# Paired heads in mixer 1, joint chunk operands and no filler matmuls in mixer 2, and a feed-forward whose last two output units run context tokens first

## The chip, the cores and the metric

The kernel runs on one core of one Trainium2 chip. The metric is the device time of one execution in microseconds. Before the change the median of three runs is 2691.66 us (2684.7 to 2692.46). Each core has TensorE (PE in the profile, with PEld for its weight loads), VectorE (DVE), ScalarE (ACT), GpSimd (POOL), SyncE (SP, which here issues DMAs), and DMA engines.

## The reference, cut to what matters

The model has four kinds of layer; the depth is 2, so two are computed: layer 0 (a bidirectional Mamba-2 mixer, then a dense SwiGLU) and layer 1 (a bidirectional RWKV-7 mixer, then eight SwiGLU experts, two per token). 256 context tokens and 256 latent tokens run through the same weights; only the latent tokens are returned.

```python
# Mamba-2, per direction, chunk of 128 tokens, G=4 groups x E=8 heads x P=64
seg = cum[:, :, :, None] - cum[:, :, None, :]
decay = jnp.exp(jnp.where(lower, seg, -jnp.inf))
cb = jnp.einsum('bcign,bcjgn->bcijg', cm, bm)
w = cb[..., None] * decay * dt[:, :, None]
y = jnp.einsum('bcijge,bcjgep->bcigep', w, x)          # "py" in the kernel
y = y + jnp.einsum('bcign,bcgepn->bcigep', cm, s_prev) * jnp.exp(cum)[..., None]

# SwiGLU and what follows it
f = (jax.nn.silu(gu[..., :F]) * gu[..., F:]) @ w_out
x = x + m[5] * f                                       # context and latent have their own m
h = _rmsnorm(x, norm1_g[1]) * (1 + m[1]) + m[0]        # mixer 2 begins

# RWKV-7, 16 heads of 64, per direction, one token at a time in the reference
sa = jnp.einsum('bhvk,bhk->bhv', S, kk_t)
S = S * w_t - sa * b_t + v_t * k_t
y_t = jnp.einsum('bhvk,bhk->bhv', S, r_t)
```

## The kernel before, in words

Activations lie with 128 features on the partitions and 512 tokens in a row: columns 0 to 255 are context, 256 to 511 latent. A large projection takes fp32 weights from HBM (`wraw`), splits them into a high and a low part (ACT cast, L206; a subtraction on DVE or POOL, L207), and runs three matmuls per tile (`mm3`, L212 to L214). Every other fp32 matmul, and so each of those that this change touches, is two records in the profile. The instructions are written as Python loops and coroutines (`weave` takes turns among them); a scheduler then orders each engine's list by its own timeline and by when tile buffers come free. So the order of the loops is not the order on an engine.

Mixer 1 (59 to 478 us) interleaves, group by group, the input projection of later features, the depthwise convolution on DVE (`cy`, L461), and the chunk computation in `mix`. There, for each pair of heads, `py` gets 128 x 512 values: per head and direction PE builds the segment sums (`pbc`, L542 and L543), ACT takes the exponential (`E`, L548), DVE multiplies by `cb` (`W`, L550), and four matmuls (L553) with 64 output rows add one chunk each. Before, the head is the outer loop, so sixteen records with the same half of the output stand in a row. `ZE = (G,)` sends the low splits of the z weights to POOL.

After the output projection and the first part of the feed-forward comes its second half (`hf == 1`): four output units n of 256 features, each over eleven k tiles and all 512 tokens. `Squares` then sums the squares of X, `rows` makes the row `rbx` of reciprocal root mean squares, and mixer 2's norm starts from it (L829, L830).

Mixer 2 (945 to 1657 us) has stages named for what runs together: A builds operands for chunks of 64 tokens in a direction (features with decay factors, `BK`; the Gram matrices `C`, L1077 and L1080; transposes `BT`, L1089), T inverts the triangular systems (`invert`), S scans. D0 and D1 are the directions; a first digit 0 is context (four chunks a direction), 1 is latent. Before, `BK` is two zero-padded tiles per slot, one per parity of the heads: 128 partitions by 4 by 128, of which 64 partitions carry data per half; so the writes L1060 and L1061 come in halves of 64 partitions. `invert` gets `warm=(2, 4)` in the stage A01T00: `spin` (L1116) then puts a 128 x 128 matmul whose result nobody reads between the small ones.

## Time and profile before

| | before |
|---|---|
| median of 3 runs | 2691.66 us |
| profiled execution | 2704.16 us |
| its span | 2702.3 us |
| PE busy | 2499.3 us (92%) |
| DVE busy | 2070.4 us (77%) |
| ACT busy | 1455.4 us (54%) |
| POOL busy | 416.1 us (15%) |
| mean granted clock of TensorE | 0.934 |

The profiled execution is 12.5 us above the median. Its 40 slices are 67.6 us long each. Read the page first by slices: the MoE (1658 us to the end) has PE and the DMA engines full and nothing of it is changed; the stages before it differ from one another, so every share has to be read per stage.

### The profile page before, as it was taken

The page shows a single profiled execution, that of the slowest core. Times are in us where ns is not written, and L with a number is a line of the kernel's source. Part 1 is how long each engine was busy: PE and PEld are TensorE (multiplying, and loading weights), DVE is VectorE, ACT ScalarE, POOL GpSimd, SP SyncE. Part 2 cuts the span into 40 slices and gives each one's busy share as a digit, 9 for nine tenths or more (in the row PEclk, how much of TensorE's full clock was granted, in tenths as well). Part 3 has the DMA queues.
Part 4 walks back from the last instruction along what each step waited for, and adds up shares of the span by engine and source line. Part 5 has one row for each costly group of instructions (what it writes and reads, how often), then busy time and mean ns, then how long its engine had stood idle before and what let it go on. Part 6 is the DMA issues. An engine that isn't in the chain of part 4 may idle for free. (4 is left out here: it accounts for less than half of the span.)

```text
span 2702.3 us, 43164 instructions
## 1 busy us (share of the span) xinstructions
PE 2499.3 (92%) x16810; PEld 2043.9 (76%) x16810; DVE 2070.4 (77%) x3118; ACT 1455.4 (54%) x2290; POOL 416.1 (15%) x506
## 2 busy tenths in 40 slices
PE   7999999999999968768977898999999999999997
PEld 4777776778888867558866687788788788878875
DVE  5777788667454377778696745999899899989997
ACT  4444446333222265336343334878787778778775
POOL 1122132110000156224453221000000000000001
PEclk9999999999999978577887877999999999999998
DMA  7322231335554231012110116699899899989983
GB/s 260 114 86 88 78 102 53 132 110 196 177 196 160 65 110 48 1 42 95 41 63 10 57 34 249 262 360 362 326 372 357 330 362 368 358 320 363 372 340 152
DMA packets 99207, 511.54 MB, mean 189 GB/s; under 512 B 11648, under 2 KB 19072, under 8 KB 55216
## 3 DMA queue, kind: packets, MB, share of 16 engines
q1 hardware_dynamic: 97520, 506.52, 51.1%
q8 instruction: 134, 2.20, 0.3%
q10 hardware_dynamic: 1472, 2.16, 0.3%
q14 instruction: 81, 0.66, 0.1%
HBM read 506.54 MB, written 2.10 MB: 188 GB/s over the span
## 5 line engine op out<-in xcount | busy, mean ns | idle before, releaser
L1734 DVE TENSOR_TENSOR wlo<-wraw,whi 128x1024 fp32r<-128x1024 f32 x662 | 798.4, 1224 | 71.3 <-ACT whi L1733 50.6
L1733 ACT CAST whi<-wraw 128x1024 fp32r<-128x1024 f32 x662 | 694.3, 1051 | 209.2 <-PE gu L214 112.0
L213 PE MATMUL gu<-wlo,xg 128*128 128x512 f32 x896 | 355.7, 397 | 1.5 <-DVE wlo L1734 0.7
L214 PE MATMUL gu<-whi,xg 128*128 128x512 f32 x896 | 350.3, 391 | 0.0
L212 PE MATMUL gu<-whi,xg 128*128 128x512 f32 x896 | 336.8, 392 | 1.1 <-ACT xg L1753 0.9
L206 ACT CAST whi<-wraw 128x1024 fp32r<-128x1024 f32 (+2 forms) x126 | 129.5, 1028 | 229.8 <-PE acc L213 216.4
L207 DVE TENSOR_TENSOR wlo<-wraw,whi 128x1024 fp32r<-128x1024 f32 (+2 forms) x110 | 131.7, 1198 | 106.3 <-ACT whi L206 106.2
L213 PEld LDWEIGHTS gu<-wlo,xg 128*128 128x128 f32 x896 | 168.8, 188 | 42.4 <-DVE wlo L1734 5.8
L212 PEld LDWEIGHTS gu<-whi,xg 128*128 128x128 f32 x896 | 168.7, 188 | 38.2 <-ACT xg L1753 1.6
L214 PEld LDWEIGHTS gu<-whi,xg 128*128 128x128 f32 x896 | 168.9, 188 | 31.6
L213 PE MATMUL y<-wlo,HT 128*128 128x512 f32 x448 | 179.1, 400 | 2.3 <-DVE wlo L1734 2.1
L212 PE MATMUL y<-whi,HT 128*128 128x512 f32 x448 | 177.1, 397 | 3.0 <-DVE xg L1754 3.0
L214 PE MATMUL y<-whi,HT 128*128 128x512 f32 x448 | 176.8, 395 | 0.0
L1808 POOL TENSOR_TENSOR wraw<-yx,SH 128x512 f32<-128x512 f32 x4 | 7.5, 1879 | 1025.4 <-DVE yx L1804 1025.4
L212 PE MATMUL acc<-h2hi,whi 128*128 128x512 f32 x352 | 137.3, 393 | 3.4 <-ACT h2hi L343 3.4
L213 PE MATMUL acc<-h2lo,whi 128*128 128x512 f32 x352 | 137.7, 391 | 0.0
L212 PE MATMUL acc<-hhi,whi 128*128 128x512 f32 (+1 forms) x328 | 135.8, 414 | 0.8 <-ACT whi L206 0.8
L214 PE MATMUL acc<-h2hi,wlo 128*128 128x512 f32 x352 | 135.0, 391 | 0.9 <-DVE wlo L207 0.9
L213 PE MATMUL acc<-hlo,whi 128*128 128x512 f32 (+1 forms) x328 | 134.1, 409 | 0.0
L214 PE MATMUL acc<-hhi,wlo 128*128 128x512 f32 (+1 forms) x328 | 133.8, 409 | 0.0
L305 POOL TENSOR_TENSOR sqa<-sqa,sq 128x512 f32<-128x512 f32 (+1 forms) x35 | 46.8, 1338 | 536.0 <-issue 311.9
L777 POOL TENSOR_TENSOR wlo<-wraw,whi 128x512 fp32r<-128x512 f32 (+1 forms) x69 | 86.1, 1257 | 150.3 <-ACT whi L776 138.9
(575 smaller groups left out, 5550.6 us busy)
## 6 DMA issues: line engine op xcount, KB each, us to landing
wraw<-in_w_mi_dram SPq DMA_DIRECT2D x219, 1024.0 KB, 4.9
wraw<-in_w_mo_dram SPq DMA_DIRECT2D x112, 1024.0 KB, 4.9
wraw<-in_w_modT_dram SPq DMA_DIRECT2D x56, 512.0 KB, 4.1
wraw<-in_w_ffi_dram SPq DMA_DIRECT2D x44, 512.0 KB, 3.6
wraw<-in_w_mod_dram SPq DMA_DIRECT2D x40, 512.0 KB, 4.5
wraw<-in_w_mb_dram SPq DMA_DIRECT2D x40, 512.0 KB, 4.3
wraw<-in_w_mbo_dram SPq DMA_DIRECT2D x16, 512.0 KB, 3.5
wraw<-in_w_ffo_dram SPq DMA_DIRECT2D x16, 512.0 KB, 3.5
```

The costliest lines, as they stand in the source:

```text
L206: S.copy(hi, raw)
L207: eng[q % len(eng)].tensor_sub(lo, raw, hi.bitcast(F32))
L212: PE.matmul(o, whi, xhi, start=start, stop=False)
L213: PE.matmul(o, whi, xlo, start=False, stop=False)
L214: PE.matmul(o, wlo, xhi, start=False, stop=stop)
L305: G.tensor_add(self.acc, self.acc, sq)
L777: self.eng[self.n % len(self.eng)].tensor_sub(lo, raw, hi.bitcast(F32))
L1733: S.copy(hi, raw[:, k:k + 2, :])
L1734: V.tensor_sub(lo, raw[:, k:k + 2, :], hi.bitcast(F32))
L1808: G.tensor_mul(xf[:, tt, 512 * n:512 * n + 512], fs, fg[:, 512 * n:512 * n + 512])
```

## The change

Four things change. In `mix` the direction becomes the outer loop: for both heads `E` and `W` are computed first (four W buffers in place of two), and then, chunk by chunk, the matmuls of head 0 and head 1 alternate, one with output partitions 0 to 63 and one with 64 to 127. Besides, the z weights' low splits go to DVE. In the feed-forward the last two of the four output units run in halves: context columns of unit 2, then of unit 3, then latent columns of both; sums of squares and the row are kept per half. In mixer 2, `BK` becomes one joint tile of 128 x 4 x 2 x 64 without padding: `BK[:, :, 0]` and `[:, :, 1]` are written by one instruction each on all partitions, the Gram matmuls and the transposes work on 64 x 64 blocks (transposes become matmuls with the identity), and `dc` is written by ACT from the cumulative sum instead of copied by DVE. In `invert` the filler matmuls go.

```diff
     class Squares:
-        def __init__(self, pool, n=NT):
+        def __init__(self, pool, n=NT, tag=""):
...
-        XE, ZE = (V,), (G,)
+        XE, ZE = (V,), (V,)
...
                 py = bank("py", 1)
-                for e in range(2):
-                    h = hf + 2 * m + e
-                    for d in range(2):
+                for d in range(2):
+                    Ws = []
+                    for e in range(2):
+                        h = hf + 2 * m + e
                         pbc = bank("pbc", 2)
...
-                        W = mt.tile([128, NT], F32, name="W")
+                        W = mt.tile([128, NT], F32, name="W", bufs=4)
                         V.tensor_mul(W, E, cb)
-                        for c in range(4):
-                            sl = slice(128 * c, 128 * c + 128)
+                        Ws.append(W)
+                    for c in range(4):
+                        sl = slice(128 * c, 128 * c + 128)
+                        for e in range(2):
                             PE.matmul(py[64 * e:64 * e + 64, sl], xdt[d][:, c, 128 * m + 64 * e:128 * m + 64 * e + 64],
-                                      W[:, sl], start=d == 0 and c == 0, stop=d == 1 and c == 3,
+                                      Ws[e][:, sl], start=d == 0 and c == 0, stop=d == 1 and c == 3,
                                       skip_group_check=True)
...
-        xsq = Squares(rowp)
+        xsq = {j: Squares(ft, 256, f"_{j}") for j in range(2)}
...
-            for n in range(4):
+            for n, part in [(n, HALF) for n in range(4 if hf == 0 else 2)] + \
+                    [(n, (x,)) for x in (HALF if hf else ()) for n in (2, 3)]:
                 mod_some(2 if hf == 0 else 0)
-                o = [acc(), acc()]
-                accumulate(o, wsplit(T["w_ffo"][hf, n]), lambda k: hid[k], 0, NH)
+                ts = slice(part[0][0].start, part[-1][0].stop)
+                o = [acc()[:, ts], acc()[:, ts]]
+                accumulate(o, wsplit(T["w_ffo"][hf, n]), lambda k: [t[:, ts] for t in hid[k]], 0, NH)
...
-        xsq.rows(D, rbx)
+                if hf and n == 3:
+                    xsq[j].rows(D, rbx[:, sl])
...
+            S.activation(un.dc[d][:, :, c:c + 1], cum[:, :, end:end + 1], AF.Exp, scale=-0.3032655)
...
-            V.tensor_copy(un.dc[d][:, :, c:c + 1], Dp[:, :, last:last + 1])
...
-            for par in range(2):
-                r, b0 = ROWS[par], 64 * par
-                V.scalar_tensor_tensor(BK[par][r, :, b0:b0 + 64], ta[r, :, cl], 0.5, Di[r], op0=ALU.mult, op1=ALU.mult)
-                G.tensor_mul(BK[par][r, :, 64 - b0:128 - b0], kd[r, :, cl], Di[r])
+            V.scalar_tensor_tensor(BK[:, :, 0], ta[:, :, cl], 0.5, Di, op0=ALU.mult, op1=ALU.mult)
+            G.tensor_mul(BK[:, :, 1], kd[:, :, cl], Di)
...
+        def side(BK, par, h, z):
+            return BK[ROWS[par], h, z ^ par, :]
...
-                    if j:
-                        PE.matmul(g[par][:, h, :], BK[par][:, h, :], KR[:, h, :], start=True, stop=True)
-                    else:
-                        for z in range(2):
-                            PE.matmul(g[par][ROWS[z], h, :], BK[par][:, h, 64 * z:64 * z + 64], KR[:, h, :],
-                                      start=True, stop=True)
+                    for z in range(2):
+                        PE.matmul(g[par][ROWS[z], h, :], side(BK, par, h, z), KR[ROWS[par], h, :], start=True, stop=True)
...
-                    PE.transpose(t[par][:, 64 * h:64 * h + 64], BK[par][ROWS[par], h, :],
-                                 ident[ROWS[par], ROWS[par]])
+                    for z in range(2):
+                        PE.matmul(t[par][ROWS[z], 64 * h:64 * h + 64], side(BK, par, h, z),
+                                  ident[ROWS[par], ROWS[par]], start=True, stop=True)
...
-    def invert(tp, un, zbank, slots={}, warm=(0, 0)):
+    def invert(tp, un, zbank, slots={}):
...
-                if warm[0] and n % warm[0] == 0:
-                    spin(zb[:, 256:], zp[:, d, n, 0:16].unsqueeze(2).to_broadcast([128, 16, 8]))
...
-            weave((invert(tp, D0, misc, warm=(2, 4)), 1), *stages(tp, r01, F, D1, 1, bks, (("gr", "xu"), ("acc", "xu")), always))
+            weave((invert(tp, D0, misc), 1), *stages(tp, r01, F, D1, 1, bks, (("gr", "xu"), ("acc", "xu")), always))
```

How the order on the engines changes is shown at three places. The first is PE in mixer 1, at one `py` group (`xdt0` and `xdt1` are the two directions, the W numbers buffers of the decay products). Before:

```order
L553 MATMUL py_843<-W_852,xdt0_677 64x128 x4
L542 LDWEIGHTS ehb_316
L542 MATMUL pbc_886<-parts1_389,ehb_316 128x512
L553 MATMUL py_843<-W_866,xdt1_678 64x128 x4
L543 LDWEIGHTS identb_83
L543 MATMUL pbc_886<-maskb_85,identb_83 128x512
```

and such a group in the changed kernel, whose lines are numbered four higher there:

```order
L557 MATMUL py_761<-W_770,xdt0_677 64x128
L557 MATMUL py_761<-W_780,xdt0_677 64x128
L557 MATMUL py_761<-W_770,xdt0_677 64x128
L557 MATMUL py_761<-W_780,xdt0_677 64x128
L557 MATMUL py_761<-W_770,xdt0_677 64x128
L525 MATMUL misc_723<-xw_721,btm_586 128x256
L557 MATMUL py_761<-W_780,xdt0_677 64x128
L525 MATMUL misc_729<-xw_727,btm_586 128x256
L557 MATMUL py_761<-W_770,xdt0_677 64x128
L557 MATMUL py_761<-W_780,xdt0_677 64x128
```

Four matmuls of one head stood in a row; now the two heads (two W buffers) take turns, and two other matmuls stand between members of one direction.

The second place is PE in the inversion of D0, stage A01T00 (M and T are the solver's tiles, `cst` the identity; L1116 is the filler). Before:

```order
L1116 MATMUL ms<-T,cst 128x128
L1197 MATMUL ms<-M_9366,T 32x16 x8
L1116 MATMUL ms<-T,cst 128x128
L1197 MATMUL ms<-M_9366,T 32x16 x8
L1116 MATMUL ms<-T,cst 128x128
```

and after, where L1196 is the same solve and L1017 and L1018 are low-rank projections of direction D1:

```order
L1196 MATMUL ms<-M_9613,T 32x16 x18
L1017 MATMUL xu<-hw_7701,l_9297 128x128
L1018 MATMUL xu<-ha_7703,l_9297 128x128
L1196 MATMUL ms<-M_9613,T 32x16 x2
L1017 MATMUL xu<-hw_7702,l_9297 128x128
L1018 MATMUL xu<-ha_7704,l_9297 128x128
L1196 MATMUL ms<-M_9613,T 32x16 x13
```

The fillers are gone, and eight pairs of D1's projections, which came behind the solve, moved into its first phase.

The third place is DVE at the end of the feed-forward (`rst` and `rbx` make the norm's row, `sq` is the norm's first product). Before:

```order
L317 RECIPROCAL rst<-rst 128x4
L323 COPY rbx<-misc 128x512
L777 TENSOR_TENSOR wlo<-wraw,whi 128x512
L699 COPY rbl<-rbx 128x256
L829 TENSOR_TENSOR sq<-X,rbx 128x256 x2
```

and after, at the second (latent) half's row:

```order
L317 RECIPROCAL rst_7640<-rst_7640 128x2
L704 TENSOR_SCALAR keep<-c_7662 128x2
L709 TENSOR_TENSOR hrk<-c_7662,vec 128x128
L323 COPY rbx<-misc 128x256
L711 TENSOR_SCALAR hrk<-hrk 128x128
L832 TENSOR_SCALAR modA<-mods_93 128x8
L837 TENSOR_TENSOR sq<-X,rbx 128x256 x2
L707 COPY rbl<-rbx 128x256
```

The context half's row is made ten rows ahead of these, and the latent half's here; the norm's first product (L829, now L837) still stands behind the second `rbx`, but ahead of the copy to `rbl` and of a weight split.

## Rows read from the trace of the kernel before

**Rows 1.** the page's span, and the granted clock in 40 slices.

```profile
span 2702.3 us, 43164 instructions
...
PEclk9999999999999978577887877999999999999998
```

**Rows 2.** busy time (records) of each engine by stretch, then granted clock, DMA share, GB/s.

```profile
104.00:200.00 96.00, 95.56 (x525) 70.63 (x524) 70.27 (x125) 42.33 (x96) 18.99 (x16) 1.00 0.23 77
200.00:300.00 100.00, 100.00 (x573) 77.31 (x573) 78.02 (x140) 49.85 (x119) 25.29 (x21) 1.00 0.24 85
300.00:400.00 100.00, 99.14 (x523) 73.80 (x522) 80.28 (x126) 42.49 (x92) 27.87 (x20) 1.00 0.27 90
400.00:478.00 78.00, 69.55 (x414) 51.60 (x414) 64.01 (x119) 43.31 (x116) 19.39 (x18) 1.00 0.18 62
1034.00:1117.00 83.00, 56.64 (x702) 49.53 (x698) 73.67 (x174) 44.13 (x128) 39.59 (x61) 0.86 0.06 20
1115.40:1153.20 37.80, 37.80 (x578) 28.99 (x578) 15.44 (x29) 7.59 (x16) 7.67 (x12) 0.50 0.01 2
...
1340.00:1400.00 60.00, 46.52 (x433) 40.91 (x433) 50.43 (x94) 25.89 (x73) 37.45 (x51) 0.89 0.13 45
1428.00:1446.60 18.60, 15.35 (x559) 14.00 (x560) 5.47 (x10) 5.97 (x13) 4.77 (x11) 0.54 0.02 4
1445.00:1535.00 90.00, 75.84 (x1133) 66.23 (x1132) 62.52 (x142) 40.45 (x112) 28.47 (x46) 0.88 0.02 6
```

**Rows 3.** PE's timeline in mixer 1: start, us from first start to last end.

```profile
209.76 1.96 PE L553 MATMUL py<-W,xdt 128*64 128x128 f32 x16
```

**Rows 4.** PE's timeline in the scan of mixer 2.

```profile
1319.03 0.69 PE L1242 MATMUL acc<-Q,BT 128*64 128x64 f32 x16
```

**Rows 5.** groups of PE up to 402 us: records, busy us, mean ns.

```profile
L553 PE MATMUL py<-W,xdt 128*64 128x128 f32 x352 | 46.6, 278 | 0.0
```

**Rows 6.** groups of all engines in mixer 1, 104 to 478 us.

```profile
L461 DVE SCALAR_TENSOR_TENSOR cy<-cv,cwh,cy 128x512 f32<-128x512 f32 x80 | 69.4, 869 | 1.1
...
L553 PE MATMUL py<-W,xdt 128*64 128x128 f32 x512 | 67.7, 278 | 1.3 <-DVE xdt L511 1.3
...
L207 POOL TENSOR_TENSOR wlo<-wraw,whi 128x1024 fp32r<-128x1024 f32 x13 | 34.5, 2652 | 44.1 <-ACT whi L206 44.1
...
L207 DVE TENSOR_TENSOR wlo<-wraw,whi 128x1024 fp32r<-128x1024 f32 x21 | 26.4, 1256 | 8.2 <-ACT whi L206 8.2
```

**Rows 7.** the convolution's line: ns min/median/max.

```profile
L461 DVE SCALAR_TENSOR_TENSOR cy<-cv,cwh,cy x96: 653/748/2944, 59.4 to 401.5; 128x512 f32<-128x512 f32 x96
```

**Rows 8.** busy time by stretch, matmuls of 512 columns, then of 256.

```profile
900.00:920.00 20.00, 20.00 (x90) 16.56 (x89) 5.37 (x8) 4.38 (x6) 3.87 (x3) 1.00 0.33 107
1240.00:1245.00 5.00, 5.00 (x44) 5.00 (x44) 2.14 (x5) 2.57 (x8) 1.89 (x2) 1.00 0.35 105
```

**Rows 9.** DVE's timeline behind the feed-forward.

```profile
948.10 0.69 DVE L323 COPY rbx<-misc 128x512 f32<-128x512 f32 x1 [1.21 <-PE misc L322]
...
949.52 1.34 DVE L699 COPY rbl<-rbx 128x256 f32<-128x256 f32 x1
950.78 0.75 DVE L829 TENSOR_TENSOR sq<-X,rbx 128x256 f32<-128x256 f32 x2
```

**Rows 10.** PE's timeline there.

```profile
956.57 0.80 PE L799 MATMUL gr<-mxh,whi 128*128 128x256 f32 x2 [8.50 <-ACT mxh L866]
```

**Rows 11.** the filler matmuls' line: ns min/median/max.

```profile
L1116 PE MATMUL ms<-T,cst x32: 421/501/582, 1115.4 to 1131.8; 128*128 128x128 f32 x32
```

**Rows 12.** groups of DVE in A00, 1034 to 1117 us.

```profile
L1060 DVE SCALAR_TENSOR_TENSOR BK<-ta,cum 64x256 f32<-64x256 f32 x22 | 14.6, 663 | 1.0 <-ACT cum L1045 0.6
...
L1053 DVE COPY dc<-Dp 128x4 f32<-128x4 f32 x11 | 4.2, 385 | 0.0
```

**Rows 13.** groups of A10 to S10A11, 1340 to 1535 us.

```profile
L1060 DVE SCALAR_TENSOR_TENSOR BK<-ta,cum 64x256 f32<-64x256 f32 x30 | 17.3, 576 | 0.4
...
L1053 DVE COPY dc<-Dp 128x4 f32<-128x4 f32 x15 | 7.9, 525 | 1.2 <-ACT Dp L1044 1.2
```

More of the change, by code (lines that the diff above doesn't have):

```diff
@@ L287, in tile_backbone @@
     class Squares:
-        def __init__(self, pool, n=NT):
-            self.pool, self.n, self.first, self.late = pool, n, True, []
-            self.acc = pool.tile([128, n], F32, name="sqa")
+        def __init__(self, pool, n=NT, tag=""):
+            self.pool, self.n, self.first, self.late, self.tag = pool, n, True, [], tag
+            self.acc = pool.tile([128, n], F32, name="sqa" + tag)
         def add(self, src, late=False):
@@ L299, in add @@
                 return
-            sq = self.pool.tile([128, self.n], F32, name="sq", bufs=2)
+            sq = self.pool.tile([128, self.n], F32, name="sq" + self.tag, bufs=2)
             S.activation(sq, src, AF.Square)
@@ L314, in rows @@
                               stop=i == len(parts) - 1, skip_group_check=True)
-            r = self.pool.tile([128, n], F32, name="rst")
+            r = self.pool.tile([128, n], F32, name="rst" + self.tag)
             S.activation(r, ss[:, :n], AF.Sqrt, scale=1.0 / width, bias=epsc)
@@ L661, in tile_backbone @@
                 hid.append((hi, lo))
-            for n in range(4):
+            for n, part in [(n, HALF) for n in range(4 if hf == 0 else 2)] + \
+                    [(n, (x,)) for x in (HALF if hf else ()) for n in (2, 3)]:
                 mod_some(2 if hf == 0 else 0)
-                o = [acc(), acc()]
-                accumulate(o, wsplit(T["w_ffo"][hf, n]), lambda k: hid[k], 0, NH)
+                ts = slice(part[0][0].start, part[-1][0].stop)
+                o = [acc()[:, ts], acc()[:, ts]]
+                accumulate(o, wsplit(T["w_ffo"][hf, n]), lambda k: [t[:, ts] for t in hid[k]], 0, NH)
                 for m in range(2):
-                    for sl, j in HALF:
-                        V.scalar_tensor_tensor(X[:, 2 * n + m, sl], o[m][:, sl], mcol(0, 5, 2 * n + m, j),
-                                               X[:, 2 * n + m, sl], op0=ALU.mult, op1=ALU.add)
-                    if hf:
-                        xsq.add(X[:, 2 * n + m, :], n == 3)
-        xsq.rows(D, rbx)
+                    for sl, j in part:
+                        V.scalar_tensor_tensor(X[:, 2 * n + m, sl], o[m][:, sl.start - ts.start:sl.stop - ts.start],
+                                               mcol(0, 5, 2 * n + m, j), X[:, 2 * n + m, sl], op0=ALU.mult, op1=ALU.add)
+                        if hf:
+                            xsq[j].add(X[:, 2 * n + m, sl], n == 3)
+                if hf and n == 3:
+                    xsq[j].rows(D, rbx[:, sl])
     dump("x2", X)
@@ L997, in stage @@
         o = 1 - d
-        last = 64 if d == 0 else 0
         gr, ms = (lambda: bank(tags[0], 2)), (lambda: bank(tags[1], 2))
@@ L1044, in decays @@
             S.activation(Dp[:, :, o:o + 64], cum, AF.Exp, scale=-0.3032655)
+            end = 63 * o
+            S.activation(un.dc[d][:, :, c:c + 1], cum[:, :, end:end + 1], AF.Exp, scale=-0.3032655)
             S.activation(cum, cum, AF.Exp, scale=0.3032655)
@@ L1112, in stage @@
             yield from grams(c, BK, 2 * i + d)
-    def spin(o, x):
-        PE.matmul(o[:, :x.shape[1] * x.shape[2]], ident, x, start=True, stop=True)
-    def invert(tp, un, zbank, slots={}, warm=(0, 0)):
+    def invert(tp, un, zbank, slots={}):
         def tile_(name, n):
@@ L1206, in invert @@
             for n in range(16):
-                if warm[1] and n % warm[1] == 0 and n < 13:
-                    spin(z[:, 32 * n:], TB[d][:, n, :].unsqueeze(2).to_broadcast([128, 32, 4]))
                 for par in range(2):
@@ L1220, in invert @@
             for n in range(16):
-                if warm[1] and n % warm[1] == 0 and n < 13:
-                    spin(z[:, 32 * n:], T32[d][:, n, :].unsqueeze(2).to_broadcast([128, 32, 4]))
                 for par in range(2):
@@ L1308, in operand_tiles @@
     def operand_tiles(tp):
-        t = [[tp.tile([128, 2, 4, 128], F32, name=f"BK{d}{i}") for i in range(2)] for d in range(2)]
-        for d in t:
-            for x in d:
-                for par in range(2):
-                    G.memset(x[:, par], 0.0)
-        return [[[x[:, par] for par in range(2)] for x in d] for d in t]
+        return [[tp.tile([128, 4, 2, 64], F32, name=f"BK{d}{i}") for i in range(2)] for d in range(2)]
     def stages(tp, rp, F, un, nb, bks, tags, ready, l2=None):
```

4 lines of the change are left out of this document (2 added, 2 removed).

## The prediction

> **What bounds the kernel now.** I read the profiled execution first by the granted clock in slices, then stage by stage in a table of windows, then single lines on the engine that the table names. The span is 2702.3 us and the execution 2704.2 [rows 1]. The clock's slices stand at nine tenths or more everywhere but in slices of 945 to 1657 us, mixer 2, and in the last one; that is the first sign that mixer 2 is a chain of short steps and mixer 1 is not. The windows say it exactly [rows 2]. In mixer 1, from 104 to 400 us, PE is busy 95.56 of 96, 100 of 100 and 99.14 of 100 us at clock 1.00: PE itself is the bound there, and only what it executes can be shortened. DVE comes next, 70.27, 78.02 and 80.28 us. In the last 78 us of mixer 1 PE has 8.45 us free. In A00 (1034 to 1117) DVE leads with 73.67 of 83 us, PE has 56.64. In the inversion of D0 (1115.4 to 1153.2) PE is busy in all of its 37.80 us, but at clock 0.50, the lower level of 1.2 GHz, whereas the inversion of the same form for latent chunks (1428 to 1446.6) takes 18.60 us. In A10 DVE has 50.43 of 60 us; in S10A11 PE leads with 75.84 of 90, DVE has 62.52.
>
> **Paired heads.** Sixteen records of 128 columns that write the same half of the output take 1.96 us from first start to last end [rows 3]; with a duration of 0.28 for the last one (the mean, 278 ns, [rows 5]) that is 1.68/15 = 112 ns from start to start, one after the other. In mixer 2's scan, sixteen records of 64 columns that alternate between the two halves of the output take 0.69 us [rows 4]. By the column, one after the other, these would need 15 x 56 = 840 ns before the last one's own duration; all together took less, so a pair runs side by side. The layout of a pair in the changed `py` (128 rows, two times 64 output rows) is the same as there. So a pair of 128-column records should take about 112 ns and not 224: 56 ns less per record.
>
> A page of the Trainium skill speaks against it: "TensorE: Matmul & The Clock Gate", section "The mechanism" (part 3), says that a weight load overlaps running matmuls only where its row group is another one (or where it goes to the background buffer), and the two heads use the same rows. By that rule nothing would be gained; the scan's pairs share their rows too and still overlap [rows 4], so I give the rule the weight of a rival, C.
>
> There are 256 such matmuls, 512 records, 352 of them up to 402 us [rows 5], where PE is the bound: 352 x 56 ns = 19.7 us. The other 160 records (9.0 us) lie where PE has 8.45 us free, and I count them at nothing. What could eat the gain is DVE. It gets sixteen low splits of 128x1024 from POOL at 1.26 us: 20.1 us more [rows 6]. In return the convolution on DVE should be disturbed less: its mean in mixer 1 is 869 ns [rows 6], its median 748 [rows 7], and 80 x 0.121 = 9.7 us come back if the splits on POOL (2652 ns each) are what holds it. Up to 400 us DVE is busy 228.6 of 296 us; with the full 20.1 it would be 248.7 of the 276 that remain, 90%. It fits, narrowly. Term: -20 us, with ends 0 (DVE or ACT's exponentials decide in place of PE) and -28.7 (all 512 records count). For both heads' E and W PE has to wait longer before a group, but the scheduler fills with projection matmuls as before, and four W buffers hold both heads of both directions.
>
> **The feed-forward's end.** 132 matmuls of 512 columns become 264 of 256. 90 of the first take 20.00 us, 44 of the second 5.00 [rows 8]: 222 and 114 ns, so 264 x 0.114 - 132 x 0.222 = +0.7 us. The weights of units 2 and 3 come and are split twice; PE is full here and DVE at 5.37 of 20 us [rows 8], so this is covered. What it buys: the norm's first product starts at 950.78, 1.99 us after `rbx` was ready at 948.79, because a weight split and the copy to `rbl` (1.34 us) stand between [rows 9]. In the new order it stands in front of that copy, but still behind the second `rbx`, so the early context row doesn't start the norm early. 1.9 us go, some 0.3 from the narrower `rbx` (0.69 us for 512 columns, [rows 9]), and with 0.7 paid and another half microsecond that the shorter chains over half the columns give, the term is -2 us. Its ends: +3 (if new weights come late at a half's start) and -8.5, the whole wait of PE for the norm's output [rows 10], if the norm really ran ahead.
>
> **The inversion of D0.** The 64 filler records fall away (32 in each phase, [rows 11]). At the full clock a record of 128 columns costs 112 ns; at half the clock 224, so 64 x 0.224 = 14.3 us of PE, all of it on the path, since PE is busy throughout. The same inversion without fillers takes 18.60 us [rows 2], 19.2 less than the 37.80 here. D1's projections now stand between the solve's matmuls and keep some of that. I take -17, with ends of -12 and -24 (D1's stage behind it gets shorter as well, since part of it has moved up).
>
> A rule of the Trainium skill would have this cost time: "TensorE: Matmul & The Clock Gate", in the section "Why this matters for your kernels", advises to keep TensorE busy without gaps, so that its clock stays high. Here PE was busy in 37.80 of 37.80 us and its clock still 0.50 [rows 2], so the fillers bought no clock and their removal can't lose any.
>
> **Joint operands.** In A00, 11 of 22 STT instructions (0.663 us) and 11 copies (0.385) go from DVE: 7.3 + 4.2 = 11.5 us [rows 12], if one on 128 partitions with as many elements each is priced as the old one on 64. DVE is busy 0.89 of that window, so 10.2 us of it show if DVE is the path in the same share. In A10 to S10A11 15 of 30 at 0.576 and 15 copies at 0.525 go: 16.5 us [rows 13], at a share of (50.43 + 62.52)/150 = 0.75 12.4 us. Against that stand: 32 exponentials on ACT, which is at 44.13 of 83 us in A00 [rows 2] and so covers them; and the transposes, which become 512 records in place of 256, at 64 columns and in pairs some 8 us more of PE in all of mixer 2 (256 pairs at 64 ns, worked out from [rows 4], against half of that). The latent Gram matmuls double in number but pair up, so their time on PE stays. I take -20 for the three stages (A00 -9, A10 -6, S10A11 -5), with ends 0 and -26. The lower end is the case that PE, not DVE, is late next in S10A11.
>
> **Sum.** -20 - 2 - 17 - 20 = -59 us: 2704.2 - 59 = 2645 us for the profiled execution. That one stood 12.5 us above the median; from the median, 2691.7 - 59 = 2633 us. The MoE, PE- and DMA-bound, is not touched.
>
> **Rivals.**
> A, the pairs run, but mixer 1 isn't shortened: DVE, with 20.1 us more and the same convolution, or ACT's exponentials for two heads ahead of a group, ends last. For it: DVE at 90% by the sum above. Against it: DVE had 68 us free up to 400 us. Mixer 1 gives 0: -39, 2653 us.
> B, more comes out: all 512 records count (-28.7 in place of -20) and the norm begins with the early context row (-8.5 in place of -2): -59 - 8.7 - 6.5 = -74, 2617 us. Against it is the order of DVE's rows at the norm.
> C, pairs don't overlap at all. Then mixer 1 gives nothing, and 512 latent Gram records of 128 columns in place of 256 cost PE 256 x 112 ns = 28.7 us more in A10 to S10A11, of which half lies in PE's free 27.6 us [rows 2]: -39 + 14 = -25, 2667 us. Against it are the scan's pairs [rows 4].
> D, slower: in mixer 1 PE loses its gapless work, because a group waits for both heads' W, and the clock falls to its lower level, as it did in the inversions [rows 2]. At half the clock 10% of the 296 us that were full take 30 us more; it takes 59/296 = 20% of the stage at the lower clock to cancel all, and at 25% the time is 2692 + 15 = 2707 us. For it: mixer 2 shows the fall wherever steps wait. Against it: projections of 512 columns are there to fill, in more than half of PE's records.
>
> **How the numbers follow.** Chances: the forecast (2618 to 2648) 0.56, A 0.19, B 0.12, C 0.08, D 0.05. A difference of 0.3%, about 8 us, is what a measurement of this kernel can tell from none. Faster by more than that hold the first four cases and a part of D: 0.94; within it 0.03; slower 0.03. The range for 8 in 10: from 2610, which holds half of B, to 2662, which holds A and a little of C. Predicted: 2633 us.
>
> **What would show it.** Right: L553's successor shows sixteen records in about 1.1 us where before there were 1.96; PE still full at clock 1.00 in mixer 1, and the output projection begins some 20 us earlier; the first product of the norm stands within 0.3 us of `rbx`; the inversion of D0 takes about 20 us with PE below its span; A00 is shorter by about 9 us and DVE by 11. Wrong: sixteen in 1.9 us (C); DVE or ACT above 95% in mixer 1 with waits of PE for W (A); a granted clock below 0.9 there (D); A00 unchanged, with PE's transposes ending last.

## The result and the profile after

The changed kernel takes 2653.15 us in the median of four runs (2648.49 to 2658.69), the kernel before in the same comparison 2689.55 us (2684.7 to 2692.46): ratio 0.9867, 95% interval 0.9841 to 0.9894, or 36.4 us less where 59 were forecast. The time lies in the stated range, faster as forecast, but in part by luck: it misses the forecast's own band (2618 to 2648) by 5 us, and the range holds it because it had been drawn to hold rival A (2653). A's reason is not what happened: mixer 1 gave its full 20 us, and what is missing is missing in mixer 2.

The table gives the length of each stage, from the start of one named instruction to the next (first matmul of the output projection, of the feed-forward's first output, of mixer 2's projections, of the solve, of the scan and so on). "Before" has two columns, because the kernel before was profiled a second time (run s3 below). The last 4.5 us of each span stand behind the last of these instructions and are left out.

| stage (us) | before | before again | after | forecast | after against the mean of before |
|---|---|---|---|---|---|
| to the output projection (mixer 1) | 479.2 | 481.1 | 459.4 | -20 | -20.8 |
| output projection and first hidden units of the feed-forward | 224.7 | 225.2 | 224.2 | 0 | -0.8 |
| rest of the feed-forward, to mixer 2's first projection | 252.7 | 252.7 | 253.6 | -2 | +0.9 |
| features and A00, to the solve of D0 | 159.5 | 158.6 | 146.0 | -9 | -13.0 |
| solve of D0, to its scan | 46.7 | 46.6 | 38.2 | -17 | -8.4 |
| scan of D0, latent features, scan of D1, A10 | 265.1 | 256.9 | 265.5 | -6 | +4.5 |
| T10, S10A11, T11, S11 | 204.1 | 203.7 | 200.6 | -5 | -3.3 |
| rest of mixer 2, MoE | 1065.8 | 1062.6 | 1061.3 | 0 | -2.9 |
| sum | 2697.8 | 2687.4 | 2648.8 | -59 | -43.8 |

The profiles give -43.8, the medians -36.4; both profiled executions of the kernel before lie above its median (2704.16 and 2693.62 against 2689.55), the changed kernel's hardly (2655.44), so about 7 us of the 43.8 belong to single executions. Where the two columns of before differ, as by 8.2 us from the scan of D0 to A10, a difference of that size in one profile of the changed kernel shows little.

The page of the changed kernel, its head and the granted clock in 40 slices, against [rows 1]:

```profile
span 2653.4 us, 45251 instructions
...
PEclk9999999999999977577888797999999999999999
```

Its windows, with the columns of [rows 2] (busy time and records by engine, granted clock, DMA share, GB/s): three of mixer 1, then features and A00, the stage from D0's solve to its scan, scan of D1 with A10, T10, S10A11:

```profile
104.00:200.00 96.00, 96.00 (x583) 70.20 (x582) 75.85 (x139) 47.26 (x111) 15.31 (x15) 1.00 0.26 84
200.00:300.00 100.00, 98.58 (x582) 73.05 (x581) 80.34 (x145) 51.55 (x122) 14.96 (x16) 1.00 0.29 93
300.00:400.00 100.00, 99.20 (x582) 73.97 (x581) 83.48 (x154) 47.81 (x115) 12.04 (x14) 1.00 0.28 92
1002.00:1083.00 81.00, 57.61 (x921) 52.43 (x919) 66.19 (x157) 42.39 (x124) 35.30 (x53) 0.75 0.10 32
1083.00:1121.20 38.20, 30.97 (x870) 28.14 (x870) 19.57 (x38) 22.94 (x59) 11.41 (x24) 0.55 0.01 3
1258.90:1386.80 127.90, 98.98 (x1375) 87.50 (x1375) 91.50 (x187) 45.29 (x124) 54.13 (x74) 0.84 0.16 50
1386.80:1396.00 9.20, 5.42 (x322) 5.10 (x322) 2.78 (x6) 2.38 (x5) 1.53 (x3) 0.53 0.05 14
1396.00:1472.80 76.80, 67.87 (x1328) 58.64 (x1327) 46.87 (x87) 35.94 (x105) 21.53 (x37) 0.86 0.01 2
```

The same stage from solve to scan in the kernel before, and in it the solve alone (its first to its last matmul), then the solve alone in the changed kernel:

```profile
1116.00:1162.80 46.80, 46.27 (x739) 36.59 (x738) 19.98 (x41) 13.54 (x30) 13.21 (x28) 0.55 0.01 2
1116.10:1153.20 37.10, 37.10 (x577) 28.49 (x576) 14.74 (x29) 7.59 (x16) 7.26 (x11) 0.50 0.01 2
```

```profile
1083.00:1110.80 27.80, 22.98 (x592) 20.48 (x592) 14.75 (x26) 16.43 (x43) 6.55 (x10) 0.50 0.01 3
```

The reader is to see three things. Mixer 1 is still full at clock 1.00, so what went there went out of PE's own work. The solve of D0 is at 0.50 without fillers as it was with them, but the stage isn't free of other work: 870 records in 38.2 us where the kernel before, fillers included, has 739 in 46.8. And in the scan of D1 with A10 PE holds 1375 records at clock 0.84.

PE's timeline at one `py` group of the changed kernel, against [rows 3]:

```profile
208.70 1.31 PE L557 MATMUL py<-W,xdt 128*64 128x128 f32 x20
```

Twenty records in 1.31 us: (1.31 - 0.28)/19 = 54 ns from start to start in the mean, where it was 112. The two heads run side by side: by the single records' starts in this row, two follow each other within 6 to 7 ns (208.859 and 208.865), and the next two come 109 ns later (208.968 and 208.975). So two records run at a time; it isn't that single records follow each other faster.

### The profile page after: what moved, and what is told of

It reads as the page before. It is cut to its first block, busy times and chain, and to the rows that moved or that the text cites. A ratio compares the mean times of both kernels' runs of the same rounds, so it can differ in the third digit from the quotient of the medians.

```text
span 2653.4 us, 45251 instructions
## 1 busy us (share of the span) xinstructions
PE 2441.8 (92%) x17902; PEld 2001.6 (75%) x17902; DVE 2046.8 (77%) x3078; ACT 1465.9 (55%) x2337; POOL 343.3 (13%) x439
## 5 line engine op out<-in xcount | busy, mean ns | idle before, releaser
L206 ACT CAST whi<-wraw 128x1024 fp32r<-128x1024 f32 (+1 forms) x132 | 135.6, 1027 | 220.0 <-PE acc L213 207.2
L207 DVE TENSOR_TENSOR wlo<-wraw,whi 128x1024 fp32r<-128x1024 f32 (+1 forms) x132 | 157.9, 1197 | 107.4 <-ACT whi L206 107.1
L260 DVE SCALAR_TENSOR_TENSOR wraw<-wraw,scb 128x1024 f32<-128x1024 f32 x56 | 68.5, 1223 | 50.8 <-DMA wraw<-in_w_modT_dram 49.9
```

What stands on the lines that cost most here:

```text
L206: S.copy(hi, raw)
L207: eng[q % len(eng)].tensor_sub(lo, raw, hi.bitcast(F32))
L260: V.scalar_tensor_tensor(t, w, 0.5, scb[:, j, :], op0=ALU.mult, op1=ALU.mult, accum_out=mods[l][:, n, j:j + 1])
```

## The experiments

Each of the first four puts one part of the change alone into the kernel before.

**p1, paired heads alone.** Edit: the change's lines in `mix`, and ZE.

```diff
-        XE, ZE = (V,), (G,)
+        XE, ZE = (V,), (V,)
...
+                    for c in range(4):
+                        sl = slice(128 * c, 128 * c + 128)
+                        for e in range(2):
                             PE.matmul(py[64 * e:64 * e + 64, sl], xdt[d][:, c, 128 * m + 64 * e:128 * m + 64 * e + 64],
```

> The kernel before with the paired heads alone (and the z low splits on DVE). Theory, from the changed kernel's trace, where the output projection begins 19.8 us earlier: the pairs run side by side and PE was the bound, so -20 us (-15 to -25) against the kernel before, ratio about 0.9925, and the last yz row about 20 us earlier. Rival 1: the 19.8 us came from elsewhere or DVE ends last without the other parts: within 5 us of before. Rival 2, pairs overlap and all 512 records count: -29 us.

Measured: 2668.36 us against 2693.24, ratio 0.9913 (0.9892 to 0.9933), -24.9 us; the output projection begins at 456.4 us. The theory holds, within its bounds, and rival 1 falls. The interval's lower end is rival 2's -29; by the stage, 22.8 to 24.7 us shorter than before, it isn't reached.

**p2, no fillers alone.** Edit:

```diff
-            weave((invert(tp, D0, misc, warm=(2, 4)), 1), *stages(tp, r01, F, D1, 1, bks, (("gr", "xu"), ("acc", "xu")), always))
+            weave((invert(tp, D0, misc), 1), *stages(tp, r01, F, D1, 1, bks, (("gr", "xu"), ("acc", "xu")), always))
```

> The kernel before without the 32 filler matmuls and nothing else. The prediction's term was -17 us. Theory now, from the changed kernel's trace: direction D1's low-rank projections move into the places of the fillers, the solve of D0 then takes about 27 to 29 us and not 18.6, and what comes back behind it is little: -6 to -10 us. Rival: -17 us, the solve at about 19 us, and the rest lost through the joint operands. A second rival from the page on the clock: the fillers kept the clock up somewhere, and the kernel becomes slower than before.

Measured: 2676.76 us, ratio 0.9923 (0.9893 to 0.9953), -16.5 us. The theory that I had formed from the changed kernel's trace falls, the first rival holds: the solve takes 20.3 us where it took 37.1, and from solve to scan it is 28.2 us, 18.5 less. The second rival falls as well: the kernel became faster, and the granted clock over the solve is 0.50, the lower of its two levels, without fillers as with them. The Trainium skill, "TensorE: Matmul & The Clock Gate", "Why this matters for your kernels", advises to keep TensorE busy so that its clock stays high. The traces here don't agree for these fillers: PE was busy in 37.10 of 37.10 us at 0.50. The windows of the solve and of the stage, and the solve's first phase on PE, fillers gone, D1's projections not in it:

```profile
1113.70:1134.00 20.30, 13.56 (x541) 12.58 (x542) 17.98 (x31) 8.33 (x18) 9.51 (x14) 0.50 0.01 3
1113.70:1142.00 28.30, 21.56 (x678) 19.86 (x678) 21.89 (x41) 13.69 (x31) 13.78 (x29) 0.54 0.02 3
```

```profile
1113.71 1.91 PE L1190 MATMUL ms<-M,T 32*32 32x16 f32 x128 [5.60 <-DVE T L1180]
1115.40 0.69 PE L1190 MATMUL ms<-T,M 32*32 32x16 f32 x35
1117.09 1.47 PE L1190 MATMUL ms<-T,M 32*32 32x16 f32 x93 [1.00 <-issue]
```

128 matmuls, 256 records, in 4.8 us (1113.71 to 1118.56); with the fillers this phase took 16.4. The same phase in the changed kernel, where L1017 and L1018 are D1's projections:

```profile
1083.04 0.72 PE L1196 MATMUL ms<-M,T 32*32 32x16 f32 x36 [3.88 <-DVE T L1186]
1083.69 0.80 PE L1017 MATMUL xu<-hw,l 128*128 128x128 f32 x2
1084.27 0.64 PE L1018 MATMUL xu<-ha,l 128*128 128x128 f32 x2
1084.84 0.29 PE L1196 MATMUL ms<-M,T 32*32 32x16 f32 x4
1085.06 0.80 PE L1017 MATMUL xu<-hw,l 128*128 128x128 f32 x2
1085.65 0.63 PE L1018 MATMUL xu<-ha,l 128*128 128x128 f32 x2
1086.21 0.60 PE L1196 MATMUL ms<-M,T 32*32 32x16 f32 x26
```

From the start of a pair of projections to the solve's next matmul it is 1084.84 - 1083.69 = 1.15 us, and there are eight such pairs of lines: 9.2 us. They lengthen the phase from 4.8 to 14.2 us; whether that costs the stage anything is what q3 asks.

**p3, joint operands alone.** Edit: all of the change's lines on `BK`, `dc`, `side` and the transposes, the fillers stay.

```diff
-        t = [[tp.tile([128, 2, 4, 128], F32, name=f"BK{d}{i}") for i in range(2)] for d in range(2)]
+        return [[tp.tile([128, 4, 2, 64], F32, name=f"BK{d}{i}") for i in range(2)] for d in range(2)]
```

> The kernel before with the joint chunk operands alone (fillers stay). The prediction's terms were -9 in A00, -6 in A10, -5 in S10A11, -20 us together. Theory now: A00 gives 10 to 14 us, A10 gives nothing or takes 2 to 5 us because the transposes' 512 records and the waits among 64x64 blocks come in its path, S10A11 gives 3: together -6 to -14 us. Rival: -20 us as predicted.

Measured: 2690.56 us (ten runs) against 2693.24, ratio 0.9984 (0.9972 to 0.9997): -2.7 us, less than either expected. In its trace features and A00 take 145.1 us, 14 less than before, and the stage from solve to scan 57.2, 10.5 more. This is that stage's window:

```profile
1100.70:1157.80 57.10, 54.47 (x933) 43.94 (x932) 18.88 (x37) 22.76 (x59) 10.99 (x24) 0.56 0.01 2
```

933 records in place of the 739 of before in that stage, at 0.56: D1's projections moved in beside the fillers. What A00 gained was largely the work that left it: the two stages together give 3.9 us.

**p4, the feed-forward's halves alone.** Edit: the change's lines in `Squares` and in the loop over n.

```diff
+            for n, part in [(n, HALF) for n in range(4 if hf == 0 else 2)] + \
+                    [(n, (x,)) for x in (HALF if hf else ()) for n in (2, 3)]:
```

> The kernel before with the feed-forward's last two units in halves and nothing else. The prediction's term was -2 us. Theory now, from the changed kernel's trace, where from the feed-forward's begin to the first projection of mixer 2 it is 376.5 us against 376.2: 0 us, within the noise of 4 us of before; the norm's first product comes about 1 us earlier, and the first projection behind it waits longer by as much. Rival: -8 us, the norm's context half ahead of the latent half.

Measured: 2707.57 us, ratio 1.0053 (1.0036 to 1.0069): 14.3 us slower, which neither expected. In the trace the feed-forward's matmuls take 3.3 us more from the first of its output to the last one's end, the way from there to the norm's product 4.0 less, to the first projection 1.4 more; and then features and A00 take 168.5 us against 159.5, and the solve 51.6 against 46.7. The first difference behind the halves is mixer 2's first weights. SP's queue and ACT's first cast of these weights in the kernel before (start, length, engine):

```profile
915.75 0.90 SPq L765 DMA_DIRECT2D wraw<-in_w_k_dram  x2
944.41 0.61 SPq L685 DMA_DIRECT2D xd<-X  x1
945.06 14.76 SPq L765 DMA_DIRECT2D wraw<-in_w_k_dram  x5
```

```profile
946.58 2.16 ACT L776 CAST whi<-wraw 128x512 fp32r<-128x512 f32 x4
```

and in p4:

```profile
945.88 0.61 SPq L689 DMA_DIRECT2D xd<-X  x1
946.54 13.43 SPq L769 DMA_DIRECT2D wraw<-in_w_k_dram  x6
```

```profile
953.37 1.14 ACT L780 CAST whi<-wraw 128x512 fp32r<-128x512 f32 x2 [1.51 <-DMA wraw<-in_w_k_dram]
```

Before, two loads were out 29 us ahead of the copy of X (`xd`), which waits for the last X, and their casts fell into ACT's gap while the row was made. With the halves all loads stand behind that copy in SP's queue; the casts come at 953.37 instead of 946.58 and wait for the DMA.

**q1, the changed kernel without the halves.** Edit: the hunk of p4 undone.

> The changed kernel with the feed-forward as before (paired heads, joint operands, no fillers). Theory: the halves cost 14 us when added alone, since mixer 2's first weights (in_w_k) are then requested 30 us later and their casts collide with the norm; so without them the changed kernel gains 8 to 16 us: about 2640 us, ratio to before 0.980. Rival: in company the halves cost nothing, as the prediction's -2 us says: 2653 to 2656 us.

Measured: 2652.07 us, ratio 0.9860 (0.9828 to 0.9892), the same as the changed kernel. The theory falls, the rival holds: in company the halves cost and give nothing that the runs can tell. Features and A00 are 143.6 us without them and 146.0 with them, not 9 apart as in p4. So the parts don't add up: alone the four give -24.9, -16.5, -2.7 and +14.3, a sum of -29.8, and the whole change gives -36.4.

**q2, `xd` on ACT's queue.** Edit:

```diff
-    SY.dma_start(xd, X[:, :, 256:512])
+    S.dma_start(xd, X[:, :, 256:512])
```

> The changed kernel, with the one copy of X to DRAM (xd) issued by ACT and not by SP. In the changed kernel the first loads of in_w_k stand behind this copy in SP's queue, and the copy waits for the last X at 925 us. Theory: with the queue free the first weights arrive before the norm, their casts fall into ACT's idle time, and 3 to 8 us come back: 2645 to 2650 us. Rival 1: the loads wait for a buffer that PE reads to the end of the feed-forward; then no earlier issue and 2653 us. Rival 2: the late weights are not what costs, but the second pass over the weights in the feed-forward itself (3.6 us) and the order behind it; then the loads come early and the time stays.

Measured: 2649.19 us, ratio 0.9832 (0.9809 to 0.9854). SP's queue in this run:

```profile
917.63 26.18 SPq L773 DMA_DIRECT2D wraw<-in_w_k_dram  x7
```

The loads are out 10 us earlier than in the changed kernel (927.59 there), and from the end of the last feed-forward matmul to the solve of D0 it is 156.1 us against 156.7. So in the profile the late weights are not what costs, as rival 2 said. The median, 4 us below the changed kernel's and the lowest of all kernels run, lies where the theory had it, and the profiled execution (2656.29) is the slowest of the four; but the interval overlaps that of the changed kernel. The run beats the kernel before, isn't shown to beat the changed one, and doesn't decide between the theory and rival 2.

**q3, the solve written ahead of D1's stages.** Edit:

```diff
-            weave((invert(tp, D0, misc), 1), *stages(tp, r01, F, D1, 1, bks, (("gr", "xu"), ("acc", "xu")), always))
+            run_all(invert(tp, D0, misc))
+            weave(*stages(tp, r01, F, D1, 1, bks, (("gr", "xu"), ("acc", "xu")), always))
```

> The changed kernel, where the inversion of D0 is written ahead of the stages of D1 and not woven with them, so the scheduler may give it precedence. Theory: in the changed kernel the sixteen pairs of D1's projections stand inside the first phase of the solve, which takes 14.2 us against 4.8 in the kernel that lost only the fillers; with precedence for the solve that phase is about 5 to 8 us, the scan of D0 begins 5 to 10 us earlier, 2644 to 2648 us. Rival: D1's chain (projections, cumulative sums, Gram matrices) is what ends last, and it only starts later: the stage stays at 38 us or gets longer, 2653 us or above.

Measured: 2658.33 us, ratio 0.9874 (0.9856 to 0.9892); solve to scan 40.9 us against 38.2. The rival holds. The solve, now undisturbed, takes 14.6 us in place of 27.8, and the scan comes no sooner: 26.3 us of D1's projections, Gram blocks and transposes follow before its first matmul. The solve and what follows it:

```profile
1082.80:1097.40 14.60, 11.73 (x534) 11.31 (x537) 4.46 (x7) 4.21 (x7) 2.42 (x4) 0.50 0.02 4
1097.40:1123.70 26.30, 17.95 (x368) 15.79 (x368) 14.33 (x31) 17.93 (x54) 8.48 (x20) 0.70 0.01 2
```

So the length of this stage hangs on D1's work, wherever it stands, and not on the place of its projections inside the solve. Whether the scan has to wait for that work or only stands behind it in PE's order no run tells.

**q4, heads one after the other.** Edit, in the changed kernel:

```diff
-                    for c in range(4):
-                        sl = slice(128 * c, 128 * c + 128)
-                        for e in range(2):
+                    for e in range(2):
+                        for c in range(4):
+                            sl = slice(128 * c, 128 * c + 128)
```

> The changed kernel with the alternation alone undone: for both heads E and W first as in the change, but then all four chunks of head 0 and then all of head 1. Theory: what mixer 1 gained is that two heads' matmuls run side by side, so without alternation the records start 110 ns apart again, the output projection begins 18 to 23 us later, and the time is 2670 to 2676 us. Rival: the gain came from the order of loops, four W buffers and the splits on DVE: then 2653 us and the records' spacing changes without changing the time.

Measured: 2662.09 us, ratio 0.9883 (0.9862 to 0.9904); the output projection begins at 465.6 us, 6.2 later than in the changed kernel, not 18 to 23; theory and rival both fall. (In the seven kernels with alternating heads and the splits on DVE it begins between 456.0 and 459.4 us, so the 6 us stand out of the spread.) A stretch of PE's timeline:

```profile
207.27 2.57 PE L557 MATMUL py<-W,xdt 128*64 128x128 f32 x32
```

(2.57 - 0.28)/31 = 74 ns from start to start, between 54 and 112. By their starts the 32 records fall into four runs of eight, 109 ns from record to record within a run, and each run begins 6 ns behind the fifth record of the one before (207.767 after 207.761): the last three records of a run alternate with the first of the next, so the runs overlap in part. (The trace names no head; the runs are told apart by the spacing alone.) Over all 512 records the time to the next start on PE, each counted up to 400 ns, adds up to 64.3 us before, 56.6 here and 41.7 in the changed kernel. So the alternation is worth 15 us of PE time and 6 us of the stage. Against before, q4's mixer 1 is 14.6 us shorter, of which its `py` records give 7.7. The other 7 us come from the order of loops, the W buffers or the z splits; u1 below gives the splits little, and between the other two no run decides.

**s1, paired heads and no fillers, nothing else.** Edit: p1's and p2's lines together.

> Paired heads and no fillers, without the joint operands and without the halves. Theory: these two are all of the gain (alone -24.9 and -16.5), the joint operands and the halves add up to about nothing in company, so 2690 - 41 = about 2651 us, ratio 0.983 to 0.987, like the changed kernel (0.9867) and the one without halves (0.9860). Rival: the joint operands are worth more once the fillers are gone, since PE is free for D1's projections there; then this kernel is 8 us or more slower than the one without halves: ratio 0.989 or above.

Measured: 2660.45 us, ratio 0.9889 (0.9872 to 0.9906). The theory's ratio was 0.983 to 0.987, so it misses, and the rival's mark of 0.989 is missed by a hair; the interval holds that mark and overlaps that of q1 (0.9828 to 0.9892). The two parts give 29 us together where alone they gave 24.9 and 16.5. By stages, one profile each, the joint operands are worth 5.7 us up to D0's scan (158.3 + 29.3 = 187.6 here, 143.6 + 38.3 = 181.9 in q1). The scan of D1 with A10 is as long as in the changed kernel, without joint operands. Its window here, and in the second profile of the kernel before:

```profile
1265.90:1393.60 127.70, 98.49 (x1055) 88.41 (x1055) 99.86 (x204) 44.36 (x116) 63.95 (x88) 0.91 0.16 51
```

```profile
1303.60:1421.00 117.40, 92.45 (x1034) 82.80 (x1033) 93.52 (x196) 41.95 (x112) 62.31 (x90) 0.96 0.14 46
```

127.7 against 117.4 us for nearly the same records (1055, 1034): most of the 12 us that the two lack together.

**s2, half of the transposes as transposes.** Edit, in the changed kernel:

```diff
-                for par in range(2):
-                    for z in range(2):
-                        PE.matmul(t[par][ROWS[z], 64 * h:64 * h + 64], side(BK, par, h, z),
-                                  ident[ROWS[par], ROWS[par]], start=True, stop=True)
+                PE.transpose(t[0][:, 64 * h:64 * h + 64], BK[ROWS[0], h].rearrange("p z q -> p (z q)"),
+                             ident[ROWS[0], ROWS[0]])
+                for z in range(2):
+                    PE.matmul(t[1][ROWS[z], 64 * h:64 * h + 64], side(BK, 1, h, z),
+                              ident[ROWS[1], ROWS[1]], start=True, stop=True)
```

> The changed kernel with the transposes of the even heads done by one transpose of 64 x 128 per head in place of two fp32 matmuls of 64 x 64, so about 640 records in place of 1024 for all of them. Theory: the joint operands' gain on DVE is eaten by PE, where transposes and Gram blocks became four times as many records; then A10 (86 us against 82) loses 2 to 3 us, A00 and S10A11 as much again, 2646 to 2650 us. Rival: what ends last in A10 is the order on the engines (PE behind a Gram block that waits for DVE, DVE behind a product that waits for PE) and not the number of PE's records: 2653 us, A10 at 85 us or more.

Measured: 2668.01 us, ratio 0.9919 (0.9902 to 0.9935), slower than the changed kernel; A10 89.6 us. The theory falls: fewer records on PE made A00 (150.8 against 146.0), the solve's stage (42.5 against 38.2) and A10 longer. The rival's A10 of 85 us or more is met, its time isn't. This run puts transposes of 64 x 128 among blocks of 64 x 64. The Trainium skill, "TensorEngine Tiling (Array Packing)", "Key Properties", states that a change of the tiling mode, as against a change of tile, drains TensorE. Whether that is the cause here stays open: no run measures such a switch by itself.

**s3, the kernel before once more.** No edit.

> The kernel before, unchanged, for a second profile. Between the two profiles shown so far, stages that the change does not touch differ as well: the features of the latent tokens 97.6 against 89.2 us, the MoE 1017 against 1012, the inversion T10 12.7 against 9.2. Theory: these vary from one execution to the next of the same program, by the time that PE's clock stands at its lower level, and a second profile gives 89 to 98, 1011 to 1017 and 8 to 13 us. Rival: they belong to the program, by its order of instructions, and come out within 1 us of the first profile.

Measured: 2693.62 us. The stage of latent features in the two profiles of the same program:

```profile
1210.70:1308.30 97.60, 86.44 (x937) 76.25 (x937) 78.45 (x145) 52.84 (x121) 40.90 (x39) 0.74 0.28 93
```

```profile
1212.80:1303.60 90.80, 79.68 (x937) 70.98 (x937) 77.27 (x145) 53.45 (x121) 41.74 (x39) 0.81 0.30 100
```

The same 937 records take 97.6 us at a mean clock of 0.74 and 90.8 at 0.81. The MoE is 1017.2 and 1014.0. The theory holds for these two and falls for T10, which is 12.7 and 13.4 us here and between 7.7 and 10.0 in the one profile of every other kernel run: that seems to belong to the program.

**u1, z splits on POOL.** Edit, in the changed kernel: `ZE = (G,)` again.

> The changed kernel with the sixteen low splits of the z weights back on POOL; the heads stay paired. Theory: DVE had room for them (83.48 of 100 us at most in the changed kernel's mixer 1), and the convolution on DVE is disturbed less when they are not on POOL, so the move is worth 0 to 3 us of the 20 in mixer 1: 2653 to 2657 us, the output projection at 459 to 463 us, the convolution's mean back near 870 ns. Rival: the move is what made room: with the splits on POOL (2.65 us each) the pairs wait for their products, the output projection begins at 468 us or later and 8 us or more are lost.

Measured: 2664.71 us, ratio 0.9891 (0.9860 to 0.9921), an interval that overlaps the changed kernel's; the median is above the theory's 2653 to 2657. The output projection begins at 460.6 us, 1.2 later, as the theory had it, and the rival's 468 falls; the convolution's mean is 935 ns and not 870. (The larger part of the difference in time stands in the scan of D1, 48.1 against 41.6 us, which the splits don't touch.) The groups of mixer 1 in the changed kernel, then in u1:

```profile
L461 DVE SCALAR_TENSOR_TENSOR cy<-cv,cwh,cy 128x512 f32<-128x512 f32 x96 | 74.8, 781 | 1.1
...
L207 DVE TENSOR_TENSOR wlo<-wraw,whi 128x1024 fp32r<-128x1024 f32 x42 | 51.8, 1233 | 13.7 <-ACT whi L206 13.5
```

```profile
L461 DVE SCALAR_TENSOR_TENSOR cy<-cv,cwh,cy 128x512 f32<-128x512 f32 x95 | 88.6, 935 | 0.9
...
L207 POOL TENSOR_TENSOR wlo<-wraw,whi 128x1024 fp32r<-128x1024 f32 x16 | 40.8, 2551 | 97.7 <-ACT whi L206 89.8 <-PE misc L572 7.9
...
L207 DVE TENSOR_TENSOR wlo<-wraw,whi 128x1024 fp32r<-128x1024 f32 x26 | 33.0, 1268 | 13.1 <-ACT whi L206 11.9 <-PE pbc L564 1.2
```

The splits cost DVE 51.8 - 33.0 = 18.8 us, and the convolution gets 13.8 back (935 ns to 781): what was worked out as +20.1 and -9.7.

## Why the prediction came out as it did, step by step

- **Paired heads, -20.** Right, in size too: -20.8 in the changed kernel, 22.8 to 24.7 alone by the stage and -24.9 by the medians. The spacing of 56 ns a record came out as 54. Rival C falls: heads that share their rows overlap. C had been drawn from the Trainium skill, "TensorE: Matmul & The Clock Gate", "The mechanism", by which a weight load overlaps running matmuls only with another row group or into the background buffer. Whether that second case holds here no run tells. That the bound was PE alone is not quite so: q4 took 15 us back from PE and lost 6.
- **The feed-forward's end, -2.** Wrong by 3: +0.9. The norm's product does come 4.0 us sooner behind the last matmul and 0.1 us behind `rbx`, but the units take 3.3 more and the first projection waits 1.6 us longer. Of the 3.3, 0.7 had been counted: the 264 records take 32.0 us for 29.9, and 1.2 us go to the context half's sums and row, which now stand among them. "Covered" was right in the units, where PE has no gap, but overlooked SP's queue behind them. Alone the part costs 14.3 us, mostly in A00 and behind it; why it does so alone and not in company stays open.
- **The fillers, -17.** Right by itself: the solve 37.1 to 20.3 us, -18.5 in the stage, -16.5 in the median. In the changed kernel the stage gives -8.4, because D1's work has moved into it out of A00: 870 records where p2 has 678. The order that was shown ahead of the prediction had D1's projections there, and the prediction gave them 2 us; the stage is 10 us longer than p2's. Taking them out of the solve doesn't help (q3).
- **Joint operands in A00, -9.** The stage shows -13.0, and that number misleads: the same work of D1 left it. A00 and the solve's stage together were forecast at -26 and gave -21.4. By s1 against q1 the joint operands are worth 5.7 up to D0's scan.
- **Joint operands in A10 and S10A11, -6 and -5.** This is the step that failed: scan of D0 to A10 gave +4.5 in place of -6, S10A11 and what surrounds it -3.3, and alone the joint operands gave 2.7 us in all where 20 had been forecast. The saving of DVE's work was right: the writes of `BK` and the copies of `dc` fell from 18.8 to 7.2 us in A00 and from 25.2 to 8.3 in A10 to S10A11 (11.5 and 16.5 had been forecast). In A00 it is 12 writes at 604 ns, where [rows 12] have 22 of 663 in a like window:

```profile
L1065 DVE SCALAR_TENSOR_TENSOR BK<-ta,cum 128x256 f32<-128x256 f32 x12 | 7.2, 604 | 0.0
```

But DVE's share of a stage was taken as the share of a saving that shows, and in A10 it isn't: DVE waits there for PE and PE for DVE. DVE is busy 91.50 us of 127.9 in the changed kernel, 93.70 of 119.7 before, and PE's wait ahead of the Gram blocks grew. These are PE's groups in the two windows, before and after, then one of DVE's waits in the changed kernel (idle time ahead, and what ended it):

```profile
L1077 PE MATMUL acc<-KR,BK 128*128 128x128 f32 x64 | 9.8, 299 | 1.8 <-DVE BK L1060 1.8
L1086 PE MATMUL acc<-KR,BK 64*64 64x128 f32 x128 | 10.3, 418 | 8.8 <-DVE BK L1065 5.8 <-DVE C L1089 2.9
```

```profile
1327.70 1.29 DVE L1089 TENSOR_TENSOR C<-acc,c 128x512 f32<-128x512 f32 x2 [4.25 <-PE acc L1086]
```

In A00, too, PE's Gram blocks still wait for `BK`, 14.6 us before and 15.2 after:

```profile
L1080 PE MATMUL gr<-KR,BK 128*64 128x64 f32 x192 | 10.3, 248 | 14.6 <-DVE BK L1060 12.4 <-DVE C L1084 1.1 <-ACT Q L930 0.9
L1086 PE MATMUL gr<-KR,BK 64*64 64x64 f32 x186 | 8.0, 287 | 15.2 <-DVE BK L1065 13.2 <-DVE C L1089 1.4 <-ACT Q L938 0.5
```

One count was wrong: the transposes became 1024 records in place of 256, not 512; s2, which takes 384 of them away, was slower and not faster, so their number isn't what cost.

What lengthens the scan of D1 with A10 is not settled: 117.4 and 119.7 us before, 119.2 in p1, 120.1 in p4, but 121.1 to 138.9 in the ten kernels that lost the fillers or have joint operands, or both. Neither is needed for it, since s1 has no joint operands (127.7) and p3 keeps the fillers (123.1). The mean granted clock goes along, 0.93 to 0.96 in the first four and 0.83 to 0.91 in the ten, but doesn't order the ten (0.86 in p3, 0.91 in s1), and whether it is cause or effect no run decides.

The rivals: A named the right time for a wrong reason, DVE never above 84 us of 100 in mixer 1. B's early context row didn't start the norm. C and D fell: the records start in pairs, and the clock in mixer 1 is 1.00. (A slip in the chances: A to C and the forecast add up to 0.95, so together with a part of D they can't be 0.94.)

Adding up, against the forecast: mixer 1 -0.8, feed-forward +2.9, A00 and solve +4.6, scan of D0 to A10 +10.5, the rest of the scans +1.7, stages not touched -3.7: 15.2, from -59 to -43.8 in the profiles, and another 7.4 from single executions to the medians.

## What to carry to other kernels

Ask first whether a saving's engine is the one without gaps: here PE's 20 us in a full mixer came in full, while DVE's 16.5 us in stages where two engines wait for each other hardly showed. Two parts that are each right can share one gap: what one empties (the fillers' places), the other fills (work that became ready earlier), so read in the changed order what moves into the freed stage, and price the two stages as one. And profile the kernel before twice ahead of explaining a stage by a few microseconds.

## What the runs showed of the hardware

- fp32 matmuls of 128 rows that write different halves of the output run side by side when they alternate: starts 6 to 7 ns apart, then 109 ns to the next two; one half alone takes 109 to 112 ns a record.
- Without alternation such runs overlap in part (q4): 74 ns a record, each run of eight beginning 6 ns behind the fifth record of the one before.
- The same instructions of one program can take 90.8 or 97.6 us from one execution to the next, the mean granted clock being 0.81 or 0.74.
- The inversion of D0, chains of 32 x 32 matmuls, ran at a granted clock of 0.50 with fillers, PE busy in 37.10 of 37.10 us, and at 0.50 without them (13.56 of 20.30 us in p2, 11.73 of 14.60 in q3).
- The convolution on DVE took 935 ns in the mean with sixteen of POOL's subtractions in the same stage (u1; 892 in the kernel before, which has them too) and 781 without them (the changed kernel).
